# Two modulation chunks of a diffusion trunk as row sums on VectorE in place of products on TensorE

## The chip, the core and the metric

The kernel runs on one core of a Trainium2 chip. A core has five engines that run side by side and wait for one another through semaphores: TensorE (PE in the profile, with its weight loads as PEld), VectorE (DVE), ScalarE (ACT), GpSimd (POOL) and SyncE (SP, which here issues nearly all transfers). Each engine takes its instructions in a fixed order. The metric is the time of one execution in microseconds on the device, the median of several runs.

## The reference

A trunk of two layers works on 256 latent tokens and 256 context tokens, each with 1024 channels, in float32. What matters here, cut from the reference:

```python
for l in range(DEPTH):                               # 2
    mod = (s_lat @ w_ada[l] + b_ada[l])[:, None, :]  # s_lat = silu(c)
    sh1, sc1, g1, sh2, sc2, g2 = jnp.split(mod, 6, axis=-1)
    mod_c = s_ctx @ w_ada[l] + b_ada[l]              # s_ctx = silu(c_ctx), split likewise
    h = modulate(rmsnorm(x, norm1_g[l]), sh1, sc1)
    p = h @ w_in[l]
    ...
    x = x + g1 * gated_merge(p[..., QKV_END:], y_conv, y_attn, w_out[l])
    h2 = modulate(rmsnorm(x, norm2_g[l]), sh2, sc2)
    x = x + g2 * conv_ffn(h2, w_up[l], ffn_dw[l], ffn_dw_b[l], w_down[l])
```

The modulation is a product of two vectors (latent and context) with a matrix of 1024 x 6144 for each layer. Its 6144 results are 48 tiles of 128: tiles 0 to 7 are the shift sh1, 8 to 15 the scale sc1, 16 to 23 the gate g1, 24 to 31 sh2, 32 to 39 sc2 and 40 to 47 g2. The convolution branch has a LayerNorm over its 512 channels; each RMS norm needs a sum of squares over 1024 channels.

## The kernel before, in words

Activations lie with channels on the 128 partitions and tokens along the rows, latent tokens first (256) and context tokens behind (256). Every weight is loaded as a unit of 128 x 1024 float32 (512 KB) into one of four `raw` buffers (`wparts`, `wunit`, L148 to L171). ScalarE rounds it to a high half `whi` (L158), VectorE subtracts to get a low half `wlo` (L159), four buffers each; a main product is three matmuls (`mm3`, L176 to L179): high weights with high and low activations, then low weights with high activations. `group` (L181) accumulates the products of one output tile in a PSUM bank; PSUM has four `main` banks, two `sc`, one `pt`, one `po`.

The modulation is made in two ways. In the first, a chunk of two tiles is made of products on TensorE: `ada_products` (L206) loads two units and multiplies them with the Silu'd vectors in strips of 32 columns (L200), ScalarE copies the rows out (`ada_rows`, L215 to L217, the copy is L217), and `ada_sums` (L220) turns them with two transposes (L224) and adds the parts and the bias on VectorE (L226, L228). Chunks 0 to 12 of layer 0 (tiles 0 to 25) are made so. In the second way, `ada_dots` (L250 to L263), a tile of 128 results is a transfer of 128 x 1024 weights, one row for each result, into a `raw` buffer, and one multiply-and-sum on VectorE (L261) for each of the two vectors, whose values lie across all partitions (`across`, L240: a transfer of one row to all partitions, L243, and its Silu, L245). Tiles 26 to 47 of layer 0 and all of layer 1 are made so. [...]

Work beside the main stream is written as generators: `group` calls `slot` (L84) twice when it is 512 tokens wide, in its middle and at its end, and once otherwise; each pass of `slot` moves every side generator on by one step. `ada_dots` adds `pace[0]` in each pass and brings out a tile when two sums (one for each vector) are due. So the pass in which a tile comes up follows from the paces. From the order in which instructions are written, and from the times at which a planner thinks them ready, the order on each engine is fixed when the kernel is built; `issue_after` puts an instruction behind another one on the same engine by hand.

The stretch that the change touches, in layer 0, begins when the attention is done (L802). The rows of the two vectors are loaded and Silu'd (L805), and a generator `g1` is started: chunk 8, then tiles 26 to 39. It runs beside eleven gate groups (`gate`, L609 to L617, the evacuation is L616) and beside `layer_norm` (L817), which finishes the convolution taps (L576), subtracts the mean (L832, L835), sums the squares, takes the root through TensorE (L326, L341) and GpSimd, and normalizes (L843 to L847). Then come the two branch projections, 16 groups in four units each (L869, L873); beside the first of them a second generator `g2` makes chunks 9 to 12, which must be out before the output projection (L903). In the output projection the residual (`residual`, L881 to L884) uses gate tiles 16 to 23, and its second half runs the two token streams one after the other; `g1` is finished after the first of them, ahead of the norm that uses tiles 24 to 39.

`SumSq.add` (L298) makes a square on ScalarE and adds it on VectorE (L312); only with `apart` set is the last square of a 256-wide sum made on VectorE (L304). `rstd` (L320) then sums over partitions with TensorE (L326).

Of the kernel before, what the change touches and what calls it, by code (L numbers as in the profile page):

```python
# [8 lines left out]
F32 = mybir.dt.float32  # L9
# [6 lines left out]
P = 128  # L16
# [29 lines left out]
def trunk(ctx: ExitStack, tc: tile.TileContext, xt, cvec, crow, wall, wada, params, bias_t, rope_t, out):  # L46
# [183 lines left out]

    def ada_all(chunks, rest=0):
        for l, j in chunks:
            ev = ada_rows(ada_products(l, j, "sc"))
            yield
            yield
            ada_sums(l, j, ev)
            for _ in range(rest):
                yield

    def across(pool_, s, **kw):  # L240

        t = pool_.tile([P, D], F32, name=nm("sb"), **kw)
        sp.dma_start(t, crow[s].partition_broadcast(P))  # L243
        with tc.issue_after(lastev[0].ins):
            act.activation(t, t, AF.Silu)  # L245
        return t

    pace = [1.0]

    def ada_dots(l, tiles, sb, place=lambda: None):  # L250


        left = 0
        for n in tiles:
            while left < len(sb):
                yield
                left += pace[0]
            left -= len(sb)
            r = raw_unit(wada[l, n], place())
            for s, v in enumerate(sb):  # L260
                dve.tensor_tensor_reduce(  # L261
                    tmp().bitcast(BF16), r, v, 1.0, pr(l, BADA + n, 1), ALU.mult, ALU.add, mods[l][:, n, s : s + 1]
                )  # L263
# [26 lines left out]
    class SumSq:  # L290
# [7 lines left out]
        def add(self, src, last=False):  # L298
            T = self.T
            if self.n == 0:  # L300
                act.activation(self.acc[:, :T], src, AF.Square)
            elif last and T == S and self.apart:
                q = tmp()[:, :T]
                dve.tensor_tensor(q, src, src, ALU.mult)  # L304
                self.parts.append(q)
            else:
                q = tmp()[:, :T]
                act.activation(q, src, AF.Square)
                if last and self.apart:
                    self.parts.append(q)  # L310
                else:
                    dve.tensor_tensor(self.acc[:, :T], self.acc[:, :T], q, ALU.add)  # L312
            self.n += 1
# [229 lines left out]
    for l in range(DEPTH):  # L543
# [5 lines left out]
        with ExitStack() if last else start as e1a:  # L549
# [251 lines left out]
            with ExitStack() as e1c:  # L801
                ec = e1c.enter_context(tc.tile_pool(name=f"ec{l}", bufs=1))  # L802

                if l == 0:
                    sb0 = [across(ec, s) for s in range(2)]  # L805

                    def ada_more():
                        yield from ada_all([(0, 8)])
                        yield from ada_dots(0, range(26, 40), sb0)

# [6 lines left out]
                def layer_norm():  # L817

                    while taps:
# [3 lines left out]
                        yield  # L823
                    pace[0] = 1.0
                    flat = [c.rearrange("p s t -> p (s t)") for c in cb]
# [8 lines left out]
                    for j in range(KC):  # L834
                        dve.scalar_tensor_tensor(flat[j], pm[:, :T], -1.0 / CONV, flat[j], ALU.mult, ALU.add)  # L835
                        s2.add(flat[j], j == KC - 1)
                    yield
                    yield
                    pb = yield from rstd(s2, CONV, "po")
                    for j in range(KC):  # L840
# [7 lines left out]
                        yield  # L848
                    pace[0] = 0.4

# [8 lines left out]
                if not last:  # L859
                    g2 = ada_all([(0, j) for j in range(9, 13)], 4)  # L860
                    add_side(g2)
# [40 lines left out]
                if not last:  # L902
                    finish(g2)  # L903
                sss = sum_squares(NS, S)
                if last:
# [217 lines left out]
def _ada_units(w):  # L1123
# [6 lines left out]
    u[0, :16] = w[0][:, : 2 * D].reshape(2, 4, P, 2, 8, P).transpose(4, 0, 2, 1, 3, 5).reshape(16, P, UW)  # L1130
    u[0, 16:26] = w[0].reshape(2, 4, P, 24, S).transpose(3, 0, 2, 1, 4)[8:13].reshape(10, P, UW)
    return u
# [80 lines left out]
```

## Time and profile before

| | |
|---|---|
| runs (median of 3) | 1130.77 us (1129.12 to 1131.17) |
| the profiled execution | 1129.18 us, of which the span from first to last instruction is 1127.4 |
| granted TensorE clock | 0.998 |
| VectorE row sums (L261) | 108, 1.28 us each |
| chunk 9 to 12's products | four times 16 instructions, at 269, 279, 288 and 298 us |
| last gate's evacuation | 267.7 us |

A row of a timeline has the start and the length in microseconds, the engine, the line in the kernel, the operation, out<-in, partitions x elements, and in brackets the idle time before it with what ended it. Rows that follow one another directly with the same work are merged, with a count. TensorE's matmuls overlap, so the distance of two starts tells what one costs, not its length.

### The profile page before, as it was taken

The numbers are of one execution on the slowest core, as the hardware profiler recorded it, in microseconds if no ns is written. First come the engines' busy times: TensorE is split into PE (matmuls) and PEld (weight loads), VectorE is DVE, ScalarE is ACT, GpSimd is POOL, SyncE is SP. The second block draws the span as 40 slices with busy tenths as digits, with TensorE's granted clock in tenths as the row PEclk, the third lists the DMA queues.
The fourth block names the chain that finished last, engine by engine and source line by source line (L and its number), as shares of the span: only waits on it lengthen the run. The fifth ranks groups of instructions, "written<-read, shape, count | busy, mean of one in ns | idle before, by whom it ended". The sixth has DMA issues, their size and how long they took to land.

```text
span 1127.4 us, 17780 instructions
## 1 busy us (share of the span) xinstructions
PE 1115.5 (99%) x6854; PEld 965.1 (86%) x6854; DVE 906.5 (80%) x1625; ACT 565.7 (50%) x937; POOL 17.2 (2%) x24
## 2 busy tenths in 40 slices
PE   9999999999999999999999999999999999999997
PEld 7678777787789988888888888989898999999997
DVE  4689999786778788888898555789996898988773
ACT  4347657542334543444334223544677667766642
POOL 0000000000000000000000000010000000000000
PEclk9999999999999999999999999999999999999999
DMA  8832231635734354545556656555533575665781
GB/s 325 310 100 89 92 117 38 200 99 198 248 120 145 110 170 133 184 152 155 165 181 205 214 188 197 176 194 174 154 109 120 180 247 175 187 193 182 213 274 57
DMA packets 53941, 190.83 MB, mean 169 GB/s; under 512 B 6240, under 2 KB 6496, under 8 KB 53856
## 3 DMA queue, kind: packets, MB, share of 16 engines
q1 hardware_dynamic: 53568, 189.65, 52.6%
q8 instruction: 54, 0.88, 0.3%
q14 instruction: 31, 0.25, 0.1%
q10 hardware_dynamic: 288, 0.04, 0.0%
HBM read 188.62 MB, written 1.05 MB: 168 GB/s over the span
## 4 chain that ended last, share of the span: by engine, by line
PE 85%; DVE 10%; DMA 2%; ACT 2%; issue 1%; POOL 0%; SPq 0%; DVEq 0%; ACTq 0%; POOLq 0%
PE main L177 25%; PE main L179 24%; PE main L178 24%; DVE cb L576 4%; PE main L629 4%; DVE wlo L159 2%; DMA raw<-in_wall 1%; PE sc L127 1%; PE sc L177 1%; PE sc L179 1%; PE sc L178 1%; PE po L200 1%; PE po L502 1%; DMA sb<-in_crow 1%; PE sc L430 0%
## 5 line engine op out<-in xcount | busy, mean ns | idle before, releaser
L177 PE MATMUL main<-h,whi 128*128 128x256 f32 (+1 forms) x1328 | 446.8, 337 | 0.0
L179 PE MATMUL main<-h,wlo 128*128 128x256 f32 (+1 forms) x1328 | 443.4, 335 | 0.5 <-DVE wlo L159 0.5
L178 PE MATMUL main<-h,whi 128*128 128x256 f32 (+1 forms) x1328 | 442.4, 333 | 0.0
L158 ACT CAST whi<-raw 128x1024 fp32r<-128x1024 f32 (+1 forms) x244 | 252.5, 1039 | 284.7 <-PE main L178 128.6
L159 DVE TENSOR_TENSOR wlo<-raw,whi 128x1024 fp32r<-128x1024 f32 (+1 forms) x244 | 293.7, 1209 | 113.3 <-ACT whi L158 108.6
L177 PEld LDWEIGHTS main<-h,whi 128*128 128x128 f32 x1328 | 249.5, 188 | 32.0 <-issue 3.9
L179 PEld LDWEIGHTS main<-h,wlo 128*128 128x128 f32 x1328 | 249.5, 188 | 28.9 <-DVE wlo L159 0.7
L178 PEld LDWEIGHTS main<-h,whi 128*128 128x128 f32 x1328 | 249.9, 188 | 28.1 <-issue 0.2
L576 DVE SCALAR_TENSOR_TENSOR cb<-u,par,cb 128x512 f32<-128x512 f32 (+1 forms) x240 | 140.6, 620 | 1.2
L261 DVE CUSTOM_DVE_ANT_0 t<-raw,sb,par 128x1024 bf16<-128x1024 f32 x100 | 126.9, 1280 | 1.4 <-ACT sb L245 1.2
L177 PE MATMUL main<-fh,whi 128*128 128x256 f32 (+1 forms) x386 | 123.0, 319 | 0.0
L178 PE MATMUL main<-fl,whi 128*128 128x256 f32 (+1 forms) x386 | 122.9, 319 | 0.0
L179 PE MATMUL main<-fh,wlo 128*128 128x256 f32 (+1 forms) x386 | 122.9, 318 | 0.0
L178 PEld LDWEIGHTS main<-fl,whi 128*128 128x128 f32 x386 | 72.7, 188 | 5.6
L177 PEld LDWEIGHTS main<-fh,whi 128*128 128x128 f32 x386 | 72.7, 188 | 5.6
L179 PEld LDWEIGHTS main<-fh,wlo 128*128 128x128 f32 x386 | 72.7, 188 | 5.5
L948 ACT ACTIVATE t<-main,par 128x512 f32<-128x512 f32 (+1 forms) x82 | 50.7, 669 | 35.3 <-PE main L179 35.3
L949 DVE SCALAR_TENSOR_TENSOR t<-main,par,t 128x510 f32<-128x510 f32 (+1 forms) x82 | 47.6, 616 | 8.2 <-ACT t L948 7.6
L952 DVE SCALAR_TENSOR_TENSOR t<-main,par,t 128x510 f32<-128x510 f32 (+1 forms) x82 | 46.6, 611 | 0.0
L356 ACT ACTIVATE h<-t,mod 128x256 fp32r<-128x256 f32 x56 | 25.2, 502 | 37.5 <-DVE t L355 37.4
L883 DVE SCALAR_TENSOR_TENSOR x<-main,mod,x 128x256 f32<-128x256 f32 x48 | 22.1, 480 | 23.6 <-PE main L179 23.4
L629 PE MATMUL main<-whi,h 128*128 128x512 f32 x128 | 40.6, 402 | 0.0
(217 smaller groups left out, 1198.0 us busy)
## 6 DMA issues: line engine op xcount, KB each, us to landing
raw<-in_wall SPq DMA_DIRECT2D x239, 512.0 KB, 4.2
raw<-in_wada SPq DMA_DIRECT2D x88, 512.0 KB, 4.4
bias<-in_bias_t SPq DMA_DIRECT2D x8, 640.0 KB, 4.4
row<-in_wada SPq DMA_DIRECT2D x8, 512.0 KB, 4.8
sb<-in_crow SPq DMA_DIRECT2D x5, 512.0 KB, 6.1
x<-in_xt SPq DMA_DIRECT2D x8, 256.0 KB, 4.6
raw<-in_wall SPq DMA_DIRECT2D x8, 256.0 KB, 6.8
out<-t SPq DMA_DIRECT2D x3, 256.0 KB, 2.1
```

Source lines behind the costliest of these rows:

```text
L158: act.copy(hi[:, c], r[:, c])
L159: dve.tensor_tensor(lo[:, c], r[:, c], hi[:, c].bitcast(F32), ALU.subtract)
L177: pe.matmul(ps, w[0], xh, start=start, stop=False)
L178: pe.matmul(ps, w[0], xl, start=False, stop=False)
L179: pe.matmul(ps, w[1], xh, start=False, stop=stop)
L261: dve.tensor_tensor_reduce(tmp().bitcast(BF16), r, v, 1.0, pr(l, BADA + n, 1), ALU.mult, ALU.add, mods[l][:, n, s : s + 1])
L356: high = act.activation(hi[:, c], y[:, c], AF.Identity, bias=b)
L576: dve.scalar_tensor_tensor(cb[j], src, w, cb[j], ALU.mult, ALU.add)
L629: pe.matmul(pv[t], h1[n == 1][k][:, c], w[n == 2][:, b], start=k + n == 0, stop=k == KD - 1 and n == 2)
L948: act.activation(c, pv_, AF.Identity, bias=pr(l, FDB + t, 1), scale=w[1])
L949: dve.scalar_tensor_tensor(c[:, :, 1:], pv_[:, :, : S - 1], w[0], c[:, :, 1:], ALU.mult, ALU.add)
L952: dve.scalar_tensor_tensor(c[:, :, : S - 1], pv_[:, :, 1:], w[2], c[:, :, : S - 1], ALU.mult, ALU.add)
```

## The change

Layer 0's chunks 11 and 12 (tiles 22 to 25) are no longer made of products; `g1` brings out tiles 22 to 39 as row sums, and their weights are laid out for that on the host. The paces of `g1` go from 1.0 to 1.3 when the taps are done and from 0.4 to 0.7 when the LayerNorm is done. A loop ahead of the output projection brings out `g1` until tile 24 has come up. The rows' transfers stay where they were, but their Silu is written behind chunk 8's copy of its products, and ordered behind it on ScalarE. The last square of every 256-wide sum of squares is made on VectorE, also where the parts are not kept apart; the LayerNorm's sum no longer names a last one.

```diff
-    def ada_all(chunks, rest=0):
+    def ada_all(chunks, rest=0, then=None):
         for l, j in chunks:
             ev = ada_rows(ada_products(l, j, "sc"))
+            if then:
+                then()
             yield
...
-    def across(pool_, s, **kw):
-
+    def rows(pool_, s, **kw):
         t = pool_.tile([P, D], F32, name=nm("sb"), **kw)
         sp.dma_start(t, crow[s].partition_broadcast(P))
+        return t
+
+    def silu_rows(t):
         with tc.issue_after(lastev[0].ins):
             act.activation(t, t, AF.Silu)
+
+    def across(pool_, s, **kw):
+
+        t = rows(pool_, s, **kw)
+        silu_rows(t)
         return t
...
-            elif last and T == S and self.apart:
+            elif last and T == S:
                 q = tmp()[:, :T]
                 dve.tensor_tensor(q, src, src, ALU.mult)
-                self.parts.append(q)
+                if self.apart:
+                    self.parts.append(q)
+                else:
+                    dve.tensor_tensor(self.acc[:, :T], self.acc[:, :T], q, ALU.add)
...
-                    sb0 = [across(ec, s) for s in range(2)]
+                    sb0 = [rows(ec, s) for s in range(2)]
...
-                        yield from ada_all([(0, 8)])
-                        yield from ada_dots(0, range(26, 40), sb0)
+                        yield from ada_all([(0, 8)], 0, lambda: [silu_rows(t) for t in sb0])
+                        yield from ada_dots(0, range(22, 40), sb0)
...
-                    pace[0] = 1.0
+                    pace[0] = 1.3
...
-                        s2.add(flat[j], j == KC - 1)
+                        s2.add(flat[j])
...
-                    pace[0] = 0.4
+                    pace[0] = 0.7
...
-                    g2 = ada_all([(0, j) for j in range(9, 13)], 4)
+                    g2 = ada_all([(0, j) for j in range(9, 11)], 4)
...
                 if not last:
                     finish(g2)
+                    while (0, 24) not in dotted:
+                        next(g1)
...
-    u[0, 16:26] = w[0].reshape(2, 4, P, 24, S).transpose(3, 0, 2, 1, 4)[8:13].reshape(10, P, UW)
+    u[0, 16:22] = w[0].reshape(2, 4, P, 24, S).transpose(3, 0, 2, 1, 4)[8:11].reshape(6, P, UW)
```

`dotted` is a list to which `ada_dots` appends each tile as it comes up.

More of the change, by code (lines that the diff above doesn't have):

```diff
@@ L238, in ada_all @@
                 yield
-    def across(pool_, s, **kw):
+    def rows(pool_, s, **kw):
         t = pool_.tile([P, D], F32, name=nm("sb"), **kw)
         sp.dma_start(t, crow[s].partition_broadcast(P))
+        return t
+    def silu_rows(t):
         with tc.issue_after(lastev[0].ins):
             act.activation(t, t, AF.Silu)
+    def across(pool_, s, **kw):
+        t = rows(pool_, s, **kw)
+        silu_rows(t)
         return t
-    pace = [1.0]
+    pace, dotted = [1.0], []
     def ada_dots(l, tiles, sb, place=lambda: None):
@@ L258, in ada_dots @@
             left -= len(sb)
+            dotted.append((l, n))
             r = raw_unit(wada[l, n], place())
```

## The prediction

> **What bounds the kernel now.** I read the page first, then TensorE's waits, then the stretch around the change by stages. The page's first rows:
>
> ```profile
> span 1127.4 us, 17780 instructions
> PE 1115.5 (99%) x6854; PEld 965.1 (86%) x6854; DVE 906.5 (80%) x1625; ACT 565.7 (50%) x937; POOL 17.2 (2%) x24
> ```
>
> TensorE is busy in all but 11.9 us. Of its waits (us in total, times, longest) two bear on the change:
>
> ```profile
> PE pt L224 <- ACT t L217: 1.1, 1, 1.1
> PE pt L326 <- DVE ss L312: 0.7, 2, 0.5
> ```
>
> The stages in which the change acts (stretch, its length, then busy us and instructions of TensorE, its weight loads, VectorE, ScalarE and GpSimd; then clock, DMA share, GB/s):
>
> ```profile
> 215.00:230.00 15.00, 15.00 (x65) 11.80 (x64) 5.96 (x7) 4.63 (x6) 0.00 (x0) 1.00 0.56 173
> 230.00:257.00 27.00, 27.00 (x124) 22.00 (x123) 24.93 (x39) 12.82 (x20) 1.99 (x1) 1.00 0.35 109
> 257.00:305.00 48.00, 48.00 (x257) 36.53 (x256) 29.64 (x51) 13.08 (x18) 0.00 (x0) 1.00 0.67 228
> ```
>
> Two things are to be seen. TensorE has no gap from 215 to 305 us, so work taken off it there shortens the kernel as long as nothing else becomes late. And VectorE is mostly free before 230 (5.96 of 15 us), full from 230 to 257 (24.93 of 27: the conv branch's LayerNorm is there), and loose after that. The added row sums live on VectorE's slack, so it matters in which of the three stretches they fall.
>
> **Part 1: products taken off TensorE.** What one chunk costs is read from chunk 9, by the matmuls on either side of it:
>
> ```profile
> 268.39 0.39 PE L178 MATMUL main<-ol,whi 128*128 128x512 f32 x1
> 268.62 0.40 PE L179 MATMUL main<-oh,wlo 128*128 128x512 f32 x1
> 268.95 1.07 PE L200 MATMUL sc<-raw,sil 128*32 128x256 f32 x16
> 269.95 0.50 PE L177 MATMUL main<-oh,whi 128*128 128x512 f32 x1
> 270.29 0.39 PE L178 MATMUL main<-ol,whi 128*128 128x512 f32 x1
> ```
>
> ```profile
> 272.59 0.39 PE L179 MATMUL main<-oh,wlo 128*128 128x512 f32 x1
> 272.82 0.38 PE L224 MATMUL pt<-ident,t 128*128 128x128 f32 x2
> 272.96 0.48 PE L177 MATMUL main<-oh,whi 128*128 128x512 f32 x1
> 273.28 0.40 PE L178 MATMUL main<-ol,whi 128*128 128x512 f32 x1
> ```
>
> Main matmuls start 0.23 us apart (268.39, 268.62). Two such steps, 0.46, lie between 268.62 and 270.29, where 1.67 us pass: the products cost 1.21. From 272.59 to 273.28 it is 0.69 − 0.46 = 0.23 for the two transposes. One chunk is 1.44 us; two of them (11 and 12) are 2.88, all on the path. [...] Two copies on ScalarE, four small instructions on VectorE and four transfers go with the chunks; TensorE waited for none of them, and I cost them at nothing.
>
> **Part 2: the rows' Silu behind chunk 8's copy.** Today ScalarE stands before the Silu until its rows have landed, and chunk 8's copy (L217), for which TensorE waits, is queued behind. SyncE's issue, ScalarE's rows, TensorE's rows:
>
> ```profile
> 202.27 0.90 SPq L243 DMA_DIRECT2D sb<-in_crow  x2
> ```
>
> ```profile
> 208.42 1.28 ACT L245 ACT_TABLE_LOAD   x1 [4.02 <-DMA sb<-in_crow]
> 209.72 2.01 ACT L245 ACTIVATE sb<-sb 128x1024 f32<-128x1024 f32 x2
> 211.63 0.35 ACT L217 COPY t<-sc 128x256 f32<-128x256 f32 x1
> ```
>
> ```profile
> 210.51 0.39 PE L179 MATMUL main<-h,wlo 128*128 128x512 f32 x1
> 212.03 0.44 PE L224 MATMUL pt<-ident,t 128*128 128x128 f32 x2 [1.13 <-ACT t L217]
> 212.22 0.48 PE L177 MATMUL main<-h,whi 128*128 128x512 f32 x1
> 212.54 0.39 PE L178 MATMUL main<-h,whi 128*128 128x512 f32 x1
> ```
>
> From 210.51 to 212.54 pass 2.03 us; less two steps (0.46) and the transposes (0.23) the stall is 1.34. With the copy first it runs while the rows are under way, and the 1.34 goes. The rows' two transfers stay where they are in SP's queue. Behind the 4.02 us wait the Silu, a gate's evacuation and the next weight copies stay queued on ScalarE, at most 0.35 us later than now. They are needed four gates on, so I cost that at nothing; if the cover were gone it would be 0.35.
>
> **Part 3: last squares on VectorE.** Where a sum of squares ends, its last square is queued on ScalarE behind weight copies, and TensorE waits for the sum twice, 0.7 us in all (L326 in the waits). On VectorE the square follows directly on the residual that makes its input. Bounds: 0, and 0.7 saved; I take 0.7, nearer to what the wait shows. VectorE has one instruction more at each of five places, at which weight halves may be 0.4 us later; nothing waited for a low half there.
>
> **Part 4: eight more row sums on VectorE.** Tiles 22 to 25 go to the head of the list. I counted the passes of the side generators by hand (two to each 512-wide group, from the first gate after the attention). Before, tiles 26 to 32 come up in passes 7, 9, 11, 13, 15, 17 and 22. With the new paces tiles 22 to 30 come in passes 7, 9, 11, 12, 14, 15, 17, 19 and 22, then 31 to 35 in 25, 28, 31, 34 and 36, and 36 to 39 at nearly the old places. Tile 24 is out in pass 11, so the added loop that asks for it does nothing, and gate values 22 and 23 are ready far ahead of their use.
>
> The LayerNorm takes passes 9 to 17, and the tenth gate's weights are asked for after pass 18, so all that comes up earlier has precedence on VectorE. In passes 10 to 17 there were four tiles; now there are five. How that stretch ends today, on VectorE, ScalarE and TensorE's loads:
>
> ```profile
> 239.63 1.22 DVE L159 TENSOR_TENSOR wlo<-raw,whi 128x1024 fp32r<-128x1024 f32 x1
> 242.57 2.07 DVE L843 SCALAR_TENSOR_TENSOR cb<-cb,par,po 128x512 f32<-128x512 f32 x3 [1.72 <-PE po L341]
> ```
>
> ```profile
> 245.21 1.28 DVE L261 CUSTOM_DVE_ANT_0 t<-raw,sb,par 128x1024 bf16<-128x1024 f32 x1
> 246.41 0.09 DVE L261 DVE_READ_ACCUMULATOR2_ANT mod<- 128x1 f32 x1
> ```
>
> ```profile
> 254.48 0.69 DVE L847 TENSOR_TENSOR sl<-cb,sh 128x512 fp32r<-128x512 f32 x1
> 255.09 2.35 DVE L159 TENSOR_TENSOR wlo<-raw,whi 128x1024 fp32r<-128x1024 f32 x2
> ```
>
> ```profile
> 256.50 0.60 ACT L616 ACTIVATE g<-main 128x512 f32<-128x512 f32 x1 [2.49 <-PE main L179]
> ```
>
> ```profile
> 256.54 0.19 PEld L179 LDWEIGHTS main<-h,wlo 128*128 128x128 f32 x1
> ```
>
> The ninth gate's products end just before its evacuation at 256.50. The pair of low halves at 255.09 belongs to the tenth and eleventh gates (counted along the copies of high halves, which wait for the buffers of four gates before). The first of the pair is done 1.22 us later (239.63 has one alone), at 256.31, and TensorE loads from it at 256.54: a margin of 0.23 us. One more tile ahead of it is two sums of 1.20 (245.21 to 246.41), 2.40 us. If the LayerNorm keeps its place against TensorE's work, TensorE waits 2.40 − 0.23 = 2.2 us. Queued behind the added sums on VectorE are the LayerNorm's steps and these low halves; behind TensorE's wait is everything.
>
> Bounds: 0, if the sums fall into the 1.72 us gap or behind the low half (no gain is possible: the half is not late today); above, 2.2 + 1.34 = 3.5, if the LayerNorm does not move forward with TensorE, and 1.13 more (the step of the pair: 2.35 − 1.22) = 4.6, if the ninth gate's low half, which fills the gap at 239.63, is late and lands in the full stretch. I take 2.2, by the rows just shown. The other added tiles fall into 257 to 305 us, where VectorE has 48 − 29.64 = 18 us free: nothing.
>
> **Sum.** −2.88 − 1.34 − 0.7 + 2.2 = −2.7 us against the profiled execution's 1129.18 (span 1127.4 and 1.8 around it), 1126.5. That execution lies 1.6 us under the median of the runs, so against the median it is 1130.77 − 2.7 = 1128.1.
>
> **The rivals.**
>
> *No wait.* TensorE stays the only bound: −2.88 − 1.34 − 0.7 = −4.9, 1125.9. For it: TensorE waits for no row sum today, and VectorE has 9 us free from 215 to 230. Against it: no sum that comes up inside the LayerNorm ran in those 9 us. Chance 0.17. [...]
>
> *A deeper wait.* The upper bounds, 3.5 to 4.6: −1.4 to −0.3 us, 1129.4 to 1130.5. For it are SyncE's issues:
>
> ```profile
> 222.97 0.33 SPq L145 DMA_DIRECT2D raw<-in_wada  x1
> 228.55 0.33 SPq L155 DMA_DIRECT2D raw<-in_wall  x1
> 237.00 0.33 SPq L145 DMA_DIRECT2D raw<-in_wada  x1
> 239.74 1.50 SPq L155 DMA_DIRECT2D raw<-in_wall  x2
> ```
>
> Weights and tiles share four raw buffers, and each transfer starts when one comes free. With five tiles in those passes the ninth gate's transfer (228.55) stands behind one tile more and would take the buffer that is free at 237. Chance 0.27.
>
> *Slower.* The same shortage at the tenth gate. What lies between a weight's transfer and its low half:
>
> ```profile
> L158 ACT CAST whi<-raw 128x1024 fp32r<-128x1024 f32 (+1 forms) x244 | 252.5, 1039 | 284.7 <-PE main L178 128.6
> ```
>
> ```profile
> raw<-in_wall SPq DMA_DIRECT2D x239, 512.0 KB, 4.2
> ```
>
> From issue to a usable half it is at least 4.2 + 1.04 + 1.22 = 6.5 us. If the tenth gate's transfer (239.74 now) must wait until the LayerNorm's last tile is summed, at 254.5 + 3.5 = 258, the half is there at 264.5 and not at the 255.2 at which TensorE, 1.34 ahead, wants it: a wait of 9.3, +4.4 us, 1135.2. It decides from an issue later than 256. Against it: this buffer comes from an earlier tile. Chance 0.06. [...]
>
> *The copy does not come first.* The order of instructions is planned when the kernel is built; if the Silu still goes ahead, the 1.34 stays: −1.4, 1129.4. Chance 0.05.
>
> **How the numbers follow.** The forecast has 0.45. About 0.2% (2.3 us) is what a measurement of this kernel can tell from no change. A wait between 1.2 and 3.2 makes the forecast −3.7 to −1.7, seven tenths of it beyond 2.3: 0.32 faster, 0.13 within. With the first rival faster has 0.49; within 0.2% are 0.13, the deeper wait and the copy that stays, 0.45; slower has 0.06. The range runs from the first rival, less half a microsecond of spread, 1125.3, to the end of the deeper wait and the same, 1131.0.
>
> **What would show it.** Right: two chunks fewer among the products and transposes; chunk 8's copy ahead of the Silu, and no wait of L224; ten sums in the LayerNorm's stretch in place of eight; a wait of TensorE for a low half (L179 for L159) of about 2 us near 255 us, at the ninth or tenth gate; no wait of L326. Wrong: no such wait for a low half, or one above 3.5 us, or waits for weights after 260 us.

## The result, and the profile after

The changed kernel takes 1138.38 us (median of 6 runs, 1135.03 to 1140.88) against 1129.94 for the kernel before in the same session: a ratio of 1.0062, 95% interval 1.0045 to 1.0079. A ratio, here and below, is an estimate made from the fast runs (all of these are) and not the quotient of two medians, which here would be 1.0075. Measured again in another session (c2 below) it was 1.0034 (1.0015 to 1.0053). It is slower, where the prediction had 1128.1 and a chance of 0.06 for slower.

The profiled execution took 1140.88 us. It is the slowest of its six, while the one of the kernel before (1129.18) is among its fastest, so the two traces lie 11.7 us apart where the medians lie 8.4. Its page begins:

```profile
span 1139.1 us, 17714 instructions
PE 1121.8 (98%) x6818; PEld 971.2 (85%) x6818; DVE 917.1 (81%) x1642; ACT 563.4 (49%) x930; POOL 17.2 (2%) x24
```

TensorE has 36 matmuls fewer (6818 for 6854) and yet is busy 6.3 us longer, which no wait can explain: some of its matmuls were slower. Its waits (us in total, times, longest):

```profile
PE pt L339 <- DVE ss L318: 4.3, 2, 2.9
PE main L177 <- ACT whi L158: 2.0, 1, 2.0
PE pt L339 <- DVE ss L325: 0.9, 1, 0.9
PE main L179 <- DVE wlo L159: 0.5, 1, 0.5
```

L224's wait is gone. The predicted wait for a low half near 255 us hasn't come (the last row was 0.5 us before as well). What came is a wait for a high half, and longer ones for sums of squares (L339 is the old L326, L318 the new add). Where the 11.7 us of span came in, by the same instruction in both profiled executions (the offset is how much later it is after):

| instruction | before | after | offset |
|---|---|---|---|
| a gate's evacuation, ahead of the change | 200.98 | 204.00 | +3.0 |
| last gate's evacuation | 267.67 | 270.60 | +2.9 |
| reading the sum of squares, output projection, first and second stream | 354.25, 368.98 | 358.14, 373.99 | +3.9, +5.0 |
| the same at the first layer's end, then its root's transposes | 737.88, 740.55 | 744.37, 748.21 | +6.5, +7.7 |
| the same near 935 us, then its root's transposes | 935.29, 937.31 | 945.43, 948.70 | +10.1, +11.4 |

**The start.** The first 3.0 us have nothing to do with the change. The same stretch by the windows view (stretch, length, busy times of the engines, then the granted clock), before and after:

```profile
12.00:24.00 12.00, 12.00 (x106) 8.46 (x104) 5.59 (x16) 4.54 (x10) 1.02 (x1) 1.00 0.93 350
```

```profile
12.00:24.00 12.00, 12.00 (x83) 9.53 (x81) 4.22 (x11) 3.83 (x8) 1.02 (x1) 0.72 0.74 289
```

A clock of 0.72 over 12 us is half clock for 6.8 us. In the 20 profiled executions of this study the first 200 us differ from the first of them by −0.5 to 0.7 us, or by 3.0 to 4.2; the latter in six, with and without moved chunks (the squares alone among them).

**The copy.** ScalarE's rows after:

```profile
208.22 0.38 ACT L217 COPY t<-sc 128x256 f32<-128x256 f32 x1 [0.80 <-PE sc L200]
211.22 1.28 ACT L249 ACT_TABLE_LOAD   x1 [2.62 <-DMA sb<-in_crow]
```

The copy is done while the rows are still under way, as predicted, and the offset falls by 1.3 there. The LayerNorm takes most of it back at once (1.1 us). Two row sums stand on VectorE between the adds of its sum of squares, where one stood before, and TensorE waits for the last add:

```profile
237.46 0.68 DVE L325 TENSOR_TENSOR ss<-ss,t 128x512 f32<-128x512 f32 x1
238.06 1.28 DVE L271 CUSTOM_DVE_ANT_0 t<-raw,sb,par 128x1024 bf16<-128x1024 f32 x1
239.26 0.68 DVE L325 TENSOR_TENSOR ss<-ss,t 128x512 f32<-128x512 f32 x1
240.09 1.02 PE L339 MATMUL pt<-one,ss 128*128 128x1 f32 x8 [0.92 <-DVE ss L325]
```

**The branch projections.** The rows that bear on it between 286 and 294 us, in order of time:

```profile
286.83 1.28 DVE L271 CUSTOM_DVE_ANT_0 t<-raw,sb,par 128x1024 bf16<-128x1024 f32 x1
288.03 0.08 DVE L271 DVE_READ_ACCUMULATOR2_ANT mod<- 128x1 f32 x1
288.14 0.33 SPq L155 DMA_DIRECT2D raw<-in_wall  x1
292.52 1.05 ACT L158 CAST whi<-raw 128x1024 fp32r<-128x1024 f32 x1 [2.85 <-DMA raw<-in_wall]
293.62 0.55 PE L177 MATMUL main<-sh,whi 128*128 128x512 f32 x1 [1.99 <-ACT whi L158]
```

Read it from below: TensorE stands still for a high half, ScalarE for its weights, and their transfer was issued 0.11 us after the second of a tile's two sums began to be read out (288.03). The transfer had been waiting for that tile's buffer: SyncE's last issue before it was at 284.07. What follows on TensorE is the clock:

```profile
292.00:294.00 2.00, 0.38 (x2) 0.33 (x3) 2.00 (x2) 1.05 (x1) 0.00 (x0) 0.99 0.84 221
294.00:296.00 2.00, 2.00 (x6) 1.61 (x5) 2.00 (x5) 0.94 (x1) 0.00 (x0) 0.50 0.59 195
296.00:298.00 2.00, 2.00 (x7) 1.52 (x7) 0.56 (x1) 0.48 (x2) 0.00 (x0) 0.66 0.85 254
```

After a wait of 2 us the granted clock is 0.50 for 3.4 us, with six matmuls in 2 us in place of nine, and 1.00 again from 298. The wait costs its length and some 1.5 us more. With the two chunks gone the offset should have fallen here by 2.9. By the same main matmuls it rose by 1.7, from 2.9 at 268 us to 4.65 at 310.

**The first layer's end.** The rows of SyncE, ScalarE, VectorE and TensorE before:

```profile
734.15 0.33 SPq L718 DMA_DIRECT2D rope<-in_rope_t  x1
734.40 1.05 ACT L158 CAST whi<-raw 128x1024 fp32r<-128x1024 f32 x1 [2.16 <-DMA raw<-in_wall]
736.63 0.42 DVE L312 TENSOR_TENSOR ss<-ss,t 128x256 f32<-128x256 f32 x1
737.19 0.58 PE L326 MATMUL pt<-one,ss 128*128 128x1 f32 x4 [0.23 <-DVE ss L312]
```

and after:

```profile
739.13 0.33 SPq L731 DMA_DIRECT2D rope<-in_rope_t  x1
740.43 1.05 ACT L158 CAST whi<-raw 128x1024 fp32r<-128x1024 f32 x1 [3.21 <-DMA raw<-in_wall]
741.51 1.23 DVE L159 TENSOR_TENSOR wlo<-raw,whi 128x1024 fp32r<-128x1024 f32 x1 [1.38 <-ACT whi L158]
742.66 0.42 DVE L314 TENSOR_TENSOR t<-x 128x256 f32<-128x256 f32 x1
743.11 0.42 DVE L318 TENSOR_TENSOR ss<-ss,t 128x256 f32<-128x256 f32 x1
743.68 0.58 PE L339 MATMUL pt<-one,ss 128*128 128x1 f32 x4 [1.39 <-DVE ss L318]
```

The issue of the next layer's rope table serves as a mark. A weight whose transfer was issued 3.5 us ahead of it in both is there 0.25 us behind it before and 1.30 behind it after. Its low half, the square and the add stand in a row on VectorE, and TensorE waits at their end. Of the change only the square (L314) lies near this place.

### The profile page after: what moved, and what is told of

It is laid out like the page before. It is cut to its first block, busy times and chain, and to the rows that moved or that the text cites. A ratio compares the mean times of both kernels' runs of the same rounds, so it can differ in the third digit from the quotient of the medians.

```text
span 1139.1 us, 17714 instructions
## 1 busy us (share of the span) xinstructions
PE 1121.8 (98%) x6818; PEld 971.2 (85%) x6818; DVE 917.1 (81%) x1642; ACT 563.4 (49%) x930; POOL 17.2 (2%) x24
## 4 chain that ended last, share of the span: by engine, by line
PE 82%; DVE 11%; DMA 3%; ACT 2%; issue 2%; SPq 0%; POOL 0%; DVEq 0%; ACTq 0%; POOLq 0%
PE main L177 23%; PE main L179 23%; PE main L178 23%; DVE cb L589 4%; PE main L642 4%; DMA raw<-in_wall 3%; DVE wlo L159 2%; PE sc L127 1%; PE sc L179 1%; PE sc L177 1%; PE sc L178 1%; ACT whi L158 1%; PE po L200 1%; PE po L515 1%; DVE t L271 1%
## 5 line engine op out<-in xcount | busy, mean ns | idle before, releaser
L271 DVE CUSTOM_DVE_ANT_0 t<-raw,sb,par 128x1024 bf16<-128x1024 f32 x108 | 136.7, 1278 | 4.8 <-DMA raw<-in_wada 3.8
L989 ACT CAST fh<-t 128x256 fp32r<-128x256 f32 (+1 forms) x43 | 21.9, 510 | 36.0 <-DVE t L979 35.5
```

What stands on the lines that cost most here:

```text
L271: dve.tensor_tensor_reduce(tmp().bitcast(BF16), r, v, 1.0, pr(l, BADA + n, 1), ALU.mult, ALU.add, mods[l][:, n, s : s + 1])
```

## The experiments

Each was timed beside the kernel before; ratios carry their 95% intervals. The first four take the change apart.

### The parts alone: e2, e3, e5, and all but the squares: e1

e1 is the changed kernel with these lines put back:

```diff
-            elif last and T == S:
+            elif last and T == S and self.apart:
```

> The changed kernel with the last squares back on ScalarE as before; copy order and row sums stay. Theory A (the two long waits of TensorE for a sum of squares, near 742 and 941 us of the changed profile, come from the last squares on VectorE): both waits fall back to about 0.4 and 0.7 us, the slow clock behind the second goes, and the time is 5 to 6 us under the changed kernel's 1138.4, so 1132 to 1134. Theory B (the loss comes from the row sums and the weights that are late behind them, and the squares only show it): both waits stay, and the time stays within 1 us of 1138.

e2 is the kernel before with `rows`, `silu_rows` and the reordered Silu alone:

```diff
-                        yield from ada_all([(0, 8)])
+                        yield from ada_all([(0, 8)], 0, lambda: [silu_rows(t) for t in sb0])
```

> The kernel before with only the Silu of the rows put behind chunk 8's copy. If the stall of 1.3 us at 211 us is real and nothing takes it back, TensorE's wait for the copy is gone and the time is 1.3 us below 1129.9: 1128.6. If the LayerNorm takes it back even without the added tiles, there is a wait for its sum of squares of about 1.1 us near 237 us and the time does not move.

e3 is the kernel before with the last squares on VectorE, and no more:

```diff
-            elif last and T == S and self.apart:
+            elif last and T == S:
...
+                    dve.tensor_tensor(self.acc[:, :T], self.acc[:, :T], q, ALU.add)
```

> The kernel before with only the last squares moved to VectorE. Theory A: TensorE waits about 1.5 us near 737 us and 3 us near 934 us for the sums, the clock drops behind the second, and the time is 4 to 6 us above 1129.9: 1134 to 1136. Theory B: no such waits, 1129 to 1130.

e5 is the kernel before with the two chunks moved and the new paces:

```diff
-                        yield from ada_dots(0, range(26, 40), sb0)
+                        yield from ada_dots(0, range(22, 40), sb0)
...
-                    pace[0] = 0.4
+                    pace[0] = 0.7
```

> The kernel before with only the two chunks as row sums (with the new paces). The products and transposes take 2.9 us off TensorE. If the wait for a weight near 291 us of the changed profile (2 us, with a clock at half for some 3.5 us behind it) comes from the row sums, it is here too and gives about 3.7 us back: 1130 to 1131. If it comes from the shift of the copy order, it is absent and the time is 1127.

| kernel | median us | ratio |
|---|---|---|
| e1 (no squares) | 1135.53 | 1.0028 (1.0012 to 1.0044) |
| e2 (copy order) | 1130.45 | 0.9989 (0.9975 to 1.0003) |
| e3 (squares) | 1132.40 | 1.0003 (0.9986 to 1.0019) |
| e5 (chunks) | 1134.81 | 1.0031 (1.0015 to 1.0047) |

The chunks alone, which were to bring 2.9 us, cost 0.31%. The copy order gained 1.35 us at its place, though its ratio can't be told from 1. The squares neither gain nor lose what the ratio can tell. The traces show more: in e3, and in e4 below, TensorE's offset rises by 0.9 us in the output projection, between 353 and 370 us. Half a microsecond of it is a wait for a low half, here in e4:

```profile
366.12 0.39 PE L179 MATMUL sc<-h,wlo 128*128 128x256 f32 x1 [0.52 <-DVE wlo L159]
```

Beside the chunks, where the order of work in that stretch is another, the same offset rises by 0.3 in the changed kernel and by 0.2 in e1. In e1, without the squares, TensorE waits in the branch projections all the same, and the waits for sums of squares stay:

```profile
PE pt L336 <- DVE ss L322: 3.2, 3, 1.6
PE main L177 <- ACT whi L158: 2.7, 2, 1.4
```

So the theory that square and add behind a late low half make those waits falls as the main cause. The kernel before had a median of 1132.36 us beside these four and not 1129.94, so the expected times compare by their ratios. By these e2 fits its 1.3 us, e1 has the size of theory A with the waits of theory B, and e5 costs more than expected (1.0000 to 1.0009): half clock follows twice, behind 291 and behind a wait at 741.

### Both kernels again, and the two small parts together: c1, c2, e4

c1 and c2 are the kernels before and after, unchanged. e4 is the kernel before with e2's and e3's edits together.

```diff
+                        yield from ada_all([(0, 8)], 0, lambda: [silu_rows(t) for t in sb0])
...
+            elif last and T == S:
```

> The kernel before, unchanged, beside the other kernels of this job. It shows how far the start of the kernel and the waits at the layers' ends (the sum of squares that ends the last row of a layer, near 737 and 934 us) vary without any change. If they vary by themselves, this profile's waits there differ from those of the first profile of this kernel (0.4 and 0.3 us) by 0.5 us or more, or its first 105 us by more than 0.5 us, and the ratio is 1.000 within its interval. If they belong to the change, they are again 0.2 to 0.5 us, and the first 105 us agree within 0.3 us.

> The changed kernel, unchanged, beside the others. Its three parts alone gave +0.31 per cent (the chunks), -0.11 (the copy order) and +0.03 (the squares), +0.23 in all, while the whole was +0.62 against other runs of the kernel before. If the parts add up, it is now at 1.001 to 1.004 times the kernel before. If they hurt each other (the LayerNorm's waits, which neither part alone has, cost 1 us, and each wait brings a time at half clock behind it), it stays at 1.005 to 1.008. In both cases TensorE waits 1.5 to 2.5 us near 291 us for a weight whose transfer began when a row-sum tile had given its buffer free.

> The kernel before with the copy order and the last squares on VectorE, and no chunk moved. If the chunks carry the loss, this is at 0.998 to 1.000 times the kernel before: 1.35 us gained at the copy, and 0 to 0.5 lost at the sums of squares. If the squares hurt beside the changed order (square and add behind a low half whose weight is late), it is at 1.001 to 1.004, with waits of 1.5 us or more for the sum of squares near 737 or 934 us that the copy order alone does not show.

c1 came out at 0.9991 (0.9978 to 1.0004), c2 at 1.0034 (1.0015 to 1.0053), in the range expected if the parts add up, and e4 at 1.0005 (0.9991 to 1.0019), between its two cases. On TensorE c1's trace agrees with the first one of the same kernel within 0.1 us up to 930 us, and then parts from it:

```profile
934.76 0.61 PE L326 MATMUL pt<-one,ss 128*128 128x1 f32 x4 [1.41 <-DVE ss L312]
```

```profile
936.00:938.00 2.00, 2.00 (x11) 2.00 (x10) 1.24 (x3) 1.10 (x2) 0.69 (x1) 0.50 0.98 320
```

A wait of 1.4 us at 934, and half clock behind it, come up in the unchanged kernel: 2.4 us of difference between two executions. Of after's offset near 935 us, that part is not the change's. The wait near 740, in contrast, is in none of the five traces without moved chunks so far (before, c1, e2, e3, e4) and in all with them.

### A fifth buffer: e7

e7 is e1, in which every other row-sum tile has a buffer of its own:

```diff
+                    def own():
+                        turn[0] += 1
+                        if turn[0] % 2:
+                            return None
+                        return ec.tile([P, UW], F32, tag="row", bufs=1, name=nm("row"))
...
-                        yield from ada_dots(0, range(22, 40), sb0)
+                        yield from ada_dots(0, range(22, 40), sb0, own)
```

> The changed kernel without its last squares, and with a fifth buffer, which every other row-sum tile of the conv stage and the branch projections takes instead of one of the four that the weights share. If the loss near 291 us comes from the shortage of buffers (a weight's transfer waits for the tile's second sum), that wait goes with the half clock behind it: ScalarE's first copy of that weight waits less than 1 us, TensorE does not wait from 285 to 300 us, and the last row of the branch projections ends about 3.5 us earlier than in the same kernel without the fifth buffer; 1130 to 1132.5, ratio 0.998 to 1.001. If the loss comes from VectorE's queue (low halves behind row sums) or from the transfers' share of the DMA engines, the fifth buffer changes nothing: the wait near 291 stays over 1.5 us, ratio 1.002 to 1.004.

Measured: 0.9998 (0.9985 to 1.0011), where e1 had 1.0028. The waits for a high half are gone; what TensorE still waits for in the branch projections are two low halves:

```profile
284.89 0.50 PE L179 MATMUL main<-oh,wlo 128*128 128x512 f32 x1 [0.53 <-DVE wlo L159]
292.21 0.50 PE L179 MATMUL main<-oh,wlo 128*128 128x512 f32 x1 [0.40 <-DVE wlo L159]
```

The clock stays at 1.00 through both. The shortage of buffers is shown. But the wait near 740 is still there, 1.62 us from one start to the next less a step, with 3.4 us at half clock, and with it the gain is gone.

### The tiles later: e8, e9

e8 is e1 with these rates, e9 is e7 with the same:

```diff
-                    pace[0] = 1.3
+                    pace[0] = 1.0
...
-                    pace[0] = 0.7
+                    pace[0] = 0.4
...
-                        pace[0] = 0.8
-                pace[0] = 0.3
+                        pace[0] = 1.2
+                pace[0] = 1.0
```

> The changed kernel without its last squares, with the rates of the kernel before in the conv stage and the branch projections (1.0 and 0.4 per pass), and higher ones in the output projection (1.2 and 1.0), so that the two added chunks' tiles come in the output projection in place of the branch projections. If the shortage of buffers near 291 us is made by the denser row sums there, the wait near 291 and its half clock go and the last row of the branch projections ends some 3.5 us earlier than without this edit; a wait of 0 to 2 us may come up in the output projection, from 305 to 350 us: ratio 0.998 to 1.002. If the shortage goes along with the tiles wherever they fall, waits of 2 us or more for a weight show between 305 and 350 us, and the ratio stays at 1.002 to 1.004.

> The version with the fifth buffer and these later rates together: copy first, both chunks, no last squares. With the fifth buffer alone TensorE still waited 1.26 us in the branch projections for two low halves behind row sums on VectorE. If those waits go as well, and the waits at the layers' ends stay as large as with the fifth buffer alone (1.3 and 0.5 us more than before), the ratio is 0.997 to 0.999, the best of all. If the tiles then disturb the output projection, it is 0.999 to 1.002, no better than the copy order alone (0.9989).

Both expectations missed: e8 has 1.0059 (1.0040 to 1.0078), e9 1.0053 (1.0033 to 1.0072). The wait near 291 went in e8, still with four buffers, and the two chunks brought their whole 2.9 us in the branch projections: the offset goes from −0.7 at 282 us to −3.6 at 310, and in e9 from 1.7 to −1.2. But a worse wait came in the output projection:

```profile
365.48 0.58 PE L179 MATMUL sc<-h,wlo 128*128 128x256 f32 x1 [3.88 <-DVE wlo L159]
```

```profile
366.00:370.00 4.00, 4.00 (x20) 4.00 (x20) 3.23 (x4) 0.00 (x0) 0.69 (x1) 0.50 0.79 209
```

The last row sum now ends at 354.3, the scales made from it (`gain`) follow, and the steps of the first stream's norm stand ahead of that low half on VectorE. Neither place is free: earlier the tiles take the weights' buffers, later they hold up the norm. No rate between the two was tried with both chunks.

### What a wait costs: d1, d2

The kernel before, with idle work in front of three sums of squares; d2 has `{2: 8, 3: 3, 5: 5}`.

```diff
+        for _ in range({2: 3, 3: 5, 5: 8}.get(rstds[0], 0)):
+            dve.tensor_tensor(ss.acc[:, : ss.T], ss.acc[:, : ss.T], ss.acc[:, : ss.T], ALU.max)
+        rstds[0] += 1
```

> The kernel before, with VectorE operations that change nothing (the greater of a sum and itself, 0.39 us each) in front of three sums of squares that TensorE waits for: 3 at the one near 367 us, 5 at the one near 720, 8 at the one near 887. It prices a wait of TensorE by its length. By the count of operations the waits are 1.0, 2.0 and 2.9 us. If a wait costs its length, the kernel ends 5.9 us later in its trace and the granted clock stays at 1.00 after each. If a wait of over 1.3 us brings the half clock for 3.4 us, as the traces of the chunk kernels look, the offset is about 1.0 after the first, 2.0 + 1.5 more after the second and 2.9 + 1.5 more after the third, 8.9 in all, and the granted clock is 0.50 for some microseconds behind the second and third alone. [...]

> The same three places with the lengths turned round: 8 operations near 367 us, 3 near 720, 5 near 887. If the length decides, the half clock now follows the first (2.9 us) and the third wait (2.0) and not the second (1.0), and the sum is the same, 8.9 us. If the place decides, it follows the second and the third again.

They gave 1.0056 (1.0037 to 1.0076) and 1.0073 (1.0054 to 1.0091). As a test of length against place they failed: the order of work around the added operations was planned anew, and waits of other lengths came out. d1's first long one is this:

```profile
895.94 0.49 PE L331 MATMUL pt<-one,ss 128*128 128x1 f32 x3 [1.72 <-DVE ss L327]
```

Two more, of 1.38 and 2.25 us, follow within 5 us, and half clock for 6.8 us began in the first of these, so it can't be laid to one gap. A single gap of 1.62 us at 726 in d2 was followed by none. So I counted the gaps of TensorE between two starts (less one step) from 30 to 1120 us in the 20 traces. Of 14 places with a single gap of 0.9 to 1.46 us none was followed by half clock. Of 30 places with a gap of 1.5 to 4.0 us, or several gaps close together, 20 were. Six of these 20 are the 4.0 us of e8 and e9, where the half clock began while the wait still ran, and four places with several gaps. Of the 24 single gaps of 1.5 to 3.1 us 14 were followed by half clock. It lasted 3.4 us at 15 of the 20 places and 6.8 at five, and 3.4 us of it cost 1.5 us (c1's offset goes from 0.9 to 2.4). Ten of the 24 were followed by none; why was not shown.

### The fetch of instructions: f1, f2, f3, f6

At the first layer's end the traces with two chunks show one thing that the others don't: a 16 KB transfer on the queue for instructions, q8, lies among the weights' transfers. In the trace of before the queue has 54 such fetches (0.88 MB). From one to the next pass 13.3 to 31.0 us but always 107 to 149 matmuls, 126 in the mean, so I take it, an estimate from these counts, that they carry TensorE's code. The thirtieth starts 6.44 us ahead of the rope table's issue before and, with 36 matmuls fewer, 1.08 us ahead of it after. f1 is e7 with 32 matmuls of one column more ahead of the sum near 236 us, f2 with the same ahead of the one near 887:

```diff
+        for i in range(32 if rstds[0] == 0 else 0):
+            pe.matmul(
+                pt[:, i % nt : i % nt + 1], sl(ss.parts[0], i % nt), one, start=True, stop=True,
+                skip_group_check=True,
+            )
+        rstds[0] += 1
```

> The version with the fifth buffer, and 32 matmuls of one column more in front of the sum of squares near 236 us (their results are overwritten): they bring TensorE's later instruction fetches forward by 32 matmuls, some 3.8 us at the first layer's end. If the fetch among the weights' transfers makes the wait there, the fetch now lies before the first transfer (4 us or more before the issue of the rope table), ScalarE's first copy of a weight behind it starts within 0.4 us of that issue (1.49 without the edit), the wait of 1.6 us near 740 falls below 0.6, and no half clock follows. If row sums or the position of the work make it, the copy starts 1.2 to 2.0 us behind the issue as in all traces with the chunks, and the wait stays at 1.3 to 2.2 us. The 32 matmuls cost 3 to 4 us in both cases.

> The same 32 matmuls in front of the sum of squares near 887 us, behind the first layer's end: a control with the same added work. By the fetch, the first layer's end is as with the fifth buffer alone: ScalarE's copy 1.2 to 2.0 us behind the issue of the rope table, and a wait of 1.3 to 2.2 us near 740. By this the whole is 1.3 to 3 us slower than with the matmuls early. If the added matmuls matter otherwise, the two agree at 740 us.

f1's rows, and the transfers from the first weight's issue to the rope table's:

```profile
742.74 0.33 SPq L736 DMA_DIRECT2D rope<-in_rope_t  x1
743.03 1.05 ACT L158 CAST whi<-raw 128x1024 fp32r<-128x1024 f32 x1 [2.19 <-DMA raw<-in_wall]
745.83 0.58 PE L344 MATMUL pt<-one,ss 128*128 128x1 f32 x4 [0.28 <-DVE ss L322]
```

```profile
q1 hardware_dynamic: 163, 0.60, 60.0%
```

f2's:

```profile
732.40 0.33 SPq L736 DMA_DIRECT2D rope<-in_rope_t  x1
733.68 1.05 ACT L158 CAST whi<-raw 128x1024 fp32r<-128x1024 f32 x1 [3.18 <-DMA raw<-in_wall]
736.47 0.58 PE L344 MATMUL pt<-one,ss 128*128 128x1 f32 x4 [1.26 <-DVE ss L322]
```

```profile
q1 hardware_dynamic: 167, 0.62, 62.6%
q8 instruction: 1, 0.02, 3.0%
```

The same work, f2 with the fetch and the wait, f1 with neither. The times, 1.0084 (1.0064 to 1.0105) and 1.0107 (1.0088 to 1.0126), were far above the 3 to 4 us expected for the added matmuls. Each of these is two instructions (6882 in the page for e7's 6818), so 64 were added and the fetch moved by 8.5 us instead of 3.8. And half clock followed the run of one-column matmuls for 10 us in f1 and 14 in f2. f1 at 236 to 244 us:

```profile
235.52 5.73 PE L337 MATMUL pt<-one,ss 128*128 128x1 f32 x50
```

```profile
240.00:244.00 4.00, 4.00 (x25) 4.00 (x24) 0.00 (x0) 0.00 (x0) 0.00 (x0) 0.62 0.01 4
```

f3 and f6 ask whether the fetch does it without any added row sum. f3 is the kernel before with half of the products of five chunks left out; f6 leaves chunk 8 whole (`j < 9`, `j >= 9`):

```diff
-            ada_half(ps, u, raw_unit(wada[l, 2 * j + u], place()))
+            r = raw_unit(wada[l, 2 * j + u], place())
+            if l or j < 8 or u:
+                ada_half(ps, u, r, l == 0 and j >= 8)
```

> The kernel before with half of the products of chunks 8 to 12 of layer zero left out (the rows' second halves alone), so that those modulation values are not the full sums: 40 matmuls fewer, about 3 us of TensorE less, no row sum added, every transfer kept. By the fetch, TensorE's fetches come 4 to 5 us later in the program, one lies among the transfers at the first layer's end, ScalarE's copy starts 1.2 to 2.0 us behind the issue of the rope table (0.13 to 0.31 in the five traces without the chunks), and TensorE waits 1.3 to 2.2 us near 735, so that of 3 us gained 1.3 to 3 are lost there: ratio 0.998 to 1.000. If the row sums make that wait, there is none (below 0.6 us), and the ratio is 0.996 to 0.998.

> The kernel before with half of the products of chunks 9 to 12 left out (chunk 8 whole), so that those modulation values are not the full sums: 32 matmuls fewer, about 2.4 us of TensorE less, no row sum added. TensorE's fetch at the first layer's end comes about 1 us earlier against the issue of the rope table than with 40 fewer, some 1.4 us before it. If the fetch alone makes the wait, ScalarE's copy starts 1.0 to 2.0 us behind that issue and TensorE waits 1.2 to 2.2 us near 735; ratio 0.998 to 1.001. If row sums are needed as well, the copy starts within 0.4 us, no wait over 0.6 us, ratio 0.996 to 0.9985.

f3 (0.9966, 0.9949 to 0.9983) had no wait near 735: its fetch came less than 0.5 us before the rope's issue, when the weight had nearly landed, so it said nothing on the question. In f6 the fetch came 1.3 us before: the copy started 1.00 us behind the mark, and TensorE's gap was 1.13 us (1.0006, 0.9992 to 1.0019). Over the 18 traces in which this place has the same order of work:

| fetch against the rope's issue | traces | first copy behind that issue | gap of TensorE |
|---|---|---|---|
| 3.0 to 0.5 us before | after, c2, e1, e5, e7, e8, e9, f2, f6 | 1.00 to 1.99 us | 1.13 to 2.18 us |
| elsewhere | before, c1, e2, e3, e4, f1, f3, f4, f5 | 0.12 to 0.33 us | below 0.8 us |

There is no exception, and f1 and f6 moved the fetch on purpose, out of the place and into it. In these 18 traces the place of the fetch decides. How it holds up the weight is partly shown: a weight lands in 16 pieces, and in the nine traces of the first row 15 of them are there by 0.22 us behind the rope's issue and the last one at 0.89 to 1.89, while in the others all 16 are there by 0.23. So one piece alone is late; why the fetch makes it late was not shown.

### One chunk: f4, f5

One chunk is 18 matmuls fewer in place of 36, and in f4 and f5 the fetch lies outside the 3.0 to 0.5 us ahead of the rope's issue (the table above). f4 is e7 with one chunk moved (tiles 24, 25) and paces half way between the old and the new (1.15 and 0.55), f5 is f4 without the fifth buffer:

```diff
-                        yield from ada_dots(0, range(22, 40), sb0, own)
+                        yield from ada_dots(0, range(24, 40), sb0, own)
...
-                    g2 = ada_all([(0, j) for j in range(9, 11)], 4)
+                    g2 = ada_all([(0, j) for j in range(9, 12)], 4)
```

> The version with the fifth buffer, with one chunk moved in place of two: 18 matmuls fewer, which move the fetch by some 2.7 us, to about 4 us before the issue of the rope table, before the first weight's transfer there. By the fetch no wait over 0.6 us near 738 and no half clock; then 1.3 us from the copy order and 1.4 from the chunk are kept: ratio 0.996 to 0.999, the best version. If the row sums make the wait, it is there with 0.7 us or more, and the ratio is 0.999 to 1.001.

> The version with one chunk moved, without the fifth buffer. If the shortage of buffers in the branch projections already comes with one chunk's tiles more, TensorE waits 1 to 2 us between 280 and 300 us (with 1.7 us more where the half clock follows), and the ratio is 0.999 to 1.002. If one chunk's tiles still fit into four buffers, there is no wait over 0.6 us there, and the ratio is as with the fifth buffer, 0.997 to 0.9995.

f4 has the lowest ratio of the kernels that compute the whole modulation, and is faster than the kernel before by a little: 1129.70 us, 0.9983 (0.9972 to 0.9995). From e2 (0.9989, 0.9975 to 1.0003) it can't be told. Its trace has no gap over 0.5 us from 30 to 900 us. But the sixteen products of the last remaining chunk stand in two pieces, two and fourteen, with main matmuls between. The two:

```profile
286.36 0.40 PE L178 MATMUL main<-ol,whi 128*128 128x512 f32 x1
286.69 0.62 PE L200 MATMUL sc<-raw,sil 128*32 128x256 f32 x2
287.24 0.50 PE L179 MATMUL main<-oh,wlo 128*128 128x512 f32 x1
287.58 0.39 PE L177 MATMUL main<-oh,whi 128*128 128x512 f32 x1
```

From 286.36 to 287.58 pass 1.22 us; less two steps (0.46) the two products cost 0.76, and the fourteen behind them cost 1.19, no less than a whole chunk's sixteen (1.21). f5 has 1.0003 (0.9990 to 1.0017). No wait over 0.6 us shows near 290 in f5, as its second case expected, and yet the ratio fits the first. Of the chunk's gain nothing is left (the offset is 2.6 at 282 us and 3.0 at 310): products of a remaining chunk wait 0.36 us for their weights, and stand in two pieces, ten and six, between main matmuls.

## Why the prediction was wrong

**Part 1, right in the price of a chunk, wrong in leaving the remaining ones as they were.** "Two of them (11 and 12) are 2.88": in e8 and e9, where the remaining chunks stand in TensorE's order as before, two chunks bring 2.9 us in the branch projections. In the changed kernel, in e7 and in f4 the products of one remaining chunk stand in two pieces, two and fourteen, and that costs some 0.75 us more. So f4's one chunk brings 0.7 and not 1.44 (offset −0.7 at the gates, −1.4 at 340 us), and the changed kernel's two bring 2.1. In f6 eight products in place of sixteen saved 0.44 us and so cost 0.77, as much as two do: most of the price of a piece comes with the change from main matmuls to products and back. The order on each engine is fixed when the kernel is built; the prediction took that of the remaining chunks as given.

**Part 2, right.** 1.34 forecast, 1.33 to 1.35 measured in after, e2, e4 and f4.

**Part 3, wrong in sign.** "On VectorE the square follows directly on the residual." It does not: between them stands a low half (741.51 in the rows above), and square and add both wait for it. The add comes 2.48 us behind the rope's issue before and 2.54 in c1, and 2.87 in e3 and 2.81 in e4: 0.35 us later. The release of TensorE's wait was VectorE's add, but what ended last ahead of it was that low half, not ScalarE's square. "Nothing waited for a low half there" failed too: in e4 TensorE waits 0.52 us for one at 366 us, and e3 and e4 lose 0.9 us in that stretch where 0.7 in all was to be saved.

**Part 4, the step that failed.** "The other added tiles fall into 257 to 305 us, where VectorE has 18 us free: nothing." VectorE had the time; the buffers were not there. The term put at nothing cost a wait of 2.0 us at 291 for a weight behind a row-sum tile, and 1.5 us of half clock behind it; a fifth buffer (e7) took both away. "Waits for weights after 260 us" was the prediction's own sign of being wrong. The predicted 2.2 us near 255 did not come: nine row sums and not ten ran between the LayerNorm's first step and its last, and what the extra one held up was the LayerNorm's own sum at 240, by 1.1 us, and not a low half. The rival with 0.06 named this shortage, at the tenth gate and with 9.3 us: the mechanism was right, place and size were not. I had weighed it only in the stretch where VectorE is full; the DMA share of 0.67 and 228 GB/s in the stretch from 257 to 305, in a row that I had quoted, is the densest of the three stretches.

**What no step had.** Single gaps of 1.5 to 3.1 us were followed by half clock in 14 of 24 cases, and the 2.0 us at 291, with 3.4 us of it behind them, cost 3.5; and with 36 matmuls away an instruction fetch that had started 6.44 us ahead of the mark started 1.08 us ahead of it, among the weights at the first layer's end, 1.2 us and again the half clock. Three times 1.5 us for the clock, 2.1 near 291, 1.2 and 2.4 at the two later sums, 1.1 in the LayerNorm, 0.3 in the output projection and 3.0 at the start, less 1.3 for the copy and 2.1 for the chunks, are 11.2 of the 11.7 us in that trace; 3.0 of it (the start) and most of the 2.4 came by the execution, not by the change.

**Open.** After measured 1.0062 and 1.0034, e1 1.0028: whether the squares cost anything beside the chunks isn't settled (alone they cost 0.9 us in two traces). Nor is why the wait near 934 us varies between executions (a gap of 0.65 to 3.1 us, in kernels of all kinds), or what sets the clock at the start.

## What to carry to other kernels

When work moves from a full engine to one with slack, count the buffers that it holds as well as the engine's time, and look where transfers are densest rather than where the engine is fullest. In this kernel a wait of the matmul engine cost its length and, behind 14 of 24 single gaps of 1.5 to 3.1 us, a time at half clock as well, of which 3.4 us cost 1.5. A chunk taken away also changes where the remaining ones stand in the fixed order, which took 0.75 us of its gain here. With 36 matmuls fewer a 16 KB instruction fetch some 440 us behind the last product left out came to start 1.08 us ahead of the mark in place of 6.44, so a loss far from the edit is first looked up among the transfers.

## What the runs showed of the hardware

- Half clock after single gaps of 1.5 to 3.1 us: 14 of 24, and after none of 14 of 0.9 to 1.46 us. Of the 20 places with half clock behind such gaps, the 4.0 us and several gaps close together counted in, it lasted 3.4 us at 15 and 6.8 at five.
- With 64 matmuls of one column in 8.6 us in f1 half clock came for 10.2 us, from the sixth microsecond on; with the same in f2 for 13.7.
- In the nine traces with a 16 KB fetch of instructions 0.9 to 2.6 us ahead of the mark the last of 16 pieces of a 512 KB weight landed 0.89 to 1.89 us behind it and the weight's first copy started 1.00 to 1.99 us behind it; in the other nine all 16 were there by 0.23 and the copy started at 0.12 to 0.33.
